# A conformer block on one core: convolution norm and activation through the convolution's PSUM banks, and another order of products in the first chunk

## The chip, the cores and the metric

The kernel runs on one core of a Trainium2 chip. The metric is the device time of one execution in microseconds (us), as the median of several runs. TensorE (PE) multiplies matrices out of SBUF into PSUM; ScalarE (ACT) and VectorE (DVE) read and write both; GpSimd (POOL) works in SBUF alone; SyncE (SP) issues the DMAs. PSUM has eight banks of 128 x 512 fp32 values.

## The reference

One layer on 256 positions of width 1024, all in float32:

```python
x = x + 0.5 * swiglu(rms_norm(x, ffn1_norm), ffn1_w_gate, ffn1_w_up, ffn1_w_down)
proj = rms_norm(x, mix_norm) @ w_in
conv_a, conv_b, q, k, v, gate_a, gate_b = jnp.split(proj, SPLITS, axis=-1)
u = causal_depthwise_conv(conv_a * jax.nn.sigmoid(conv_b), conv_dw, conv_dw_bias)   # 31 taps
u = jax.nn.silu(layer_norm(u, conv_ln_gain, conv_ln_bias))
y_a = u @ w_conv_proj
y_b = moba_attention(rms_norm(q), rms_norm(k), v) @ w_attn_proj      # 16 heads; 256 positions: one causal block
x = x + (jax.nn.sigmoid(gate_a) * y_a + jax.nn.sigmoid(gate_b) * y_b) @ w_out
x = x + 0.5 * swiglu(rms_norm(x, ffn2_norm), ffn2_w_gate, ffn2_w_up, ffn2_w_down)
```

## The kernel before

**Products.** Every fp32 operand is split in two fp32r parts, `hi` (rounded) and `lo` (the rest), for weights and for activations. A product of two operands is three matmuls: activation hi by weight hi (L165), activation hi by weight lo (L166), activation lo by weight hi (L167); in the first chunk, `gemm_first`, these are L132, L133 and L134. The program names the activation parts hTh and hTl, oh and ol (attention output), u2h and u2l (convolution output), mTh and mTl.

**Weights.** `gemm` makes one chunk of 512 output columns for both halves t of the 256 positions. It takes the weight in pieces of two times 128 rows: SP loads `raw` (512 KB), ACT casts it to `hi` (L100), DVE or POOL subtracts to get `lo` (L102), and PE issues 24 / 2 = 12 matmuls per piece. `raw`, `hi` and `lo` are rings of five buffers, so a load waits until `hi` and `lo` of the piece five earlier have been made. The first chunk is loaded in eight smaller pieces, each with a slice of x, which ACT (L125, hTh) and DVE (L126, hTl) scale and split.

**PSUM.** Three rings share the eight banks: `acc` (3 banks, the accumulators of `gemm`), `cv` (2) and `tr` (3, transposes and attention). In the kernel before, `cv` holds the accumulators of the first chunk and later those of the depthwise convolution, two channel blocks at a time; convolution works on DVE (L347) with its first tap on ACT (L343), and its result is copied back to `uT0` to `uT3` (L350).

**Norm and activation of the convolution.** `conv_norm` transposes `uT` to positions on partitions (16 transposes, L359, four in a bank), ACT copies each bank to `ynat` (L364), DVE takes statistics (L368, L370), ACT and POOL make the reciprocal root (L185, L187), and DVE normalizes `ynat` (L375); all this once for each half t. `conv_act` transposes back (16 transposes, L385; a bank needs both halves), ACT applies Silu with gain and bias into `z` (L392) and casts to `u2h` (L398), DVE subtracts to get `u2l` (L399).

**The order around it.** Python code is written as one sequence; `conv` and `conv_norm` are generators that `pump` advances a step at a time between weight pieces. The build's scheduler then lays the instructions out on each engine by an estimated timeline, under the data's dependencies and the rings' free buffers; each engine runs its list in order. Attention is eight blocks of `score` (L465), `flip` (L512, with copies L515) and `value` (L529, with L220 and L221 into oh and ol), all in the `tr` ring. The two chunks of `w_attn` follow, whose results are multiplied by the sigmoid of gate_b (L703, L714); then two chunks of `w_conv` (reading u2h and u2l) with gate_a (L722, L723); then `w_out` and the second feed-forward. ACT needs a table load when it changes between Exp, Sigmoid and Silu; `issue_after` keeps those groups apart: gate_b's sigmoids come after attention's last cast, the Silus after them, and gate_a's sigmoids after the instruction that `conv_act` returns.

Of the kernel before, what the change touches and what calls it, by code (L numbers as in the profile page):

```python
# [20 lines left out]
KD = D // P  # L21
# [7 lines left out]
CH = 512  # L29
# [21 lines left out]
class Build:  # L51
# [54 lines left out]
    def gemm_first(self, x0, w0, rest, hT):  # L106

        nc = self.nc
        acc = [self.cv(), self.cv()]
        hTh, hTl = hT  # L110
        ah, al = self.parts(*hT)
        for k in range(KD):
            raw = self.wp.tile([P, KP * CH], F32, tag="raw", name="raw", bufs=RAW_BUFS)
            hi = self.wp.tile([P, KP * CH], F32R, tag="hi", name="hi", bufs=HI_BUFS)
            lo = self.wp.tile([P, KP * CH], F32R, tag="lo", name="lo", bufs=LO_BUFS)
            if k == 0:
                nc.sync.dma_start(x0, self.io["x0"])
                nc.sync.dma_start(raw[:, :CH], w0)
                xk = x0[:, KD:]
            else:  # L120
                self.last_dma = nc.sync.dma_start(raw[:, : CH + S], rest[:, k - 1, :])
                xk = raw[:, CH : CH + S]
            g = x0[:, k : k + 1]
            sl = slice(k * S, (k + 1) * S)
            nc.scalar.activation(hTh[:, sl], xk, AF.Copy, scale=g)  # L125
            nc.vector.scalar_tensor_tensor(  # L126
                hTl[:, sl], xk, g, hTh[:, sl].bitcast(F32), ALU.mult, ALU.subtract
            )
            self.split(raw[:, :CH], hi[:, :CH], lo[:, :CH], False)
            for t in range(2):  # L130
                o, st, sp = acc[t], k == 0, k == KD - 1
                nc.tensor.matmul(o, ah(k, t), hi[:, :CH], start=st, stop=False)  # L132
                nc.tensor.matmul(o, ah(k, t), lo[:, :CH], start=False, stop=False)  # L133
                nc.tensor.matmul(o, al(k, t), hi[:, :CH], start=False, stop=sp)  # L134
        return acc

    def gemm(self, w, c, n, kt, ah, al, pump=0, pool=0.0, split_k=None, side=None):
# [214 lines left out]
    def conv_norm(self, yT, ynat):  # L352
        nc = self.nc
        for t in range(2):
            for c0 in range(0, KD, 4):
                ps = self.tr()
                for q in range(4):
                    c = c0 + q
                    nc.tensor.transpose(  # L359
                        ps[:, q * P : (q + 1) * P],  # L360
                        yT[c // 2][:, (c % 2) * S + t * P : (c % 2) * S + (t + 1) * P],
                        self.ident,
                    )
                nc.scalar.copy(ynat[:, t * D + c0 * P : t * D + (c0 + 4) * P], ps)  # L364
                yield 1
            st = self.tmp.tile([P, 2, 6], F32, tag="bst", name="bst", bufs=2)
            for c in range(2):
                nc.vector.bn_stats(st[:, c, :], ynat[:, t * D + c * CH : t * D + (c + 1) * CH])  # L368
            mv = self.tmp.tile([P, 2], F32, tag="mv", name="mv", bufs=2)
            nc.vector.bn_aggr(mv, st)  # L370
            r = self.rsqrt_mean(mv[:, 1:2], 1, 1)
            yield 1
            for c in range(2):
                y = ynat[:, t * D + c * CH : t * D + (c + 1) * CH]
                nc.vector.tensor_scalar(y, y, mv[:, 0:1], r, ALU.subtract, ALU.mult)  # L375
            yield 1

    def conv_act(self, ynat, hi, lo, after):
        nc = self.nc
        cst = self.cst  # L380
        for c in range(0, KD, 2):
            ps = self.tr()
            for q in range(2):
                for t in range(2):
                    nc.tensor.transpose(  # L385
                        ps[:, q * S + t * P : q * S + (t + 1) * P],
                        ynat[:, t * D + (c + q) * P : t * D + (c + q + 1) * P], self.ident,
                    )
            z = self.tmp.tile([P, CH], F32, tag="junk", name="z", bufs=2)
            with self.tc.issue_after(after.ins):  # L390
                for q in range(2):
                    last = nc.scalar.activation(  # L392
                        z[:, q * S : (q + 1) * S], ps[:, q * S : (q + 1) * S], AF.Silu,
                        bias=cst[:, C_LB + c + q : C_LB + c + q + 1],
                        scale=cst[:, C_LG + c + q : C_LG + c + q + 1],
                    )
            h = hi[:, c * S : (c + 2) * S]
            nc.scalar.copy(h, z)  # L398
            nc.vector.tensor_tensor(lo[:, c * S : (c + 2) * S], z, h.bitcast(F32), ALU.subtract)  # L399
        return last  # L400


    def head_norm(self, acc, rstd, c, dst, gain, rq=None):
# [437 lines left out]
```

## Time and profile before

| | |
|---|---|
| median of 3 runs | 647.08 us (646.92 to 647.13) |
| profiled execution | 647.48 us, its span 645.6 us |
| busy share of PE, DVE, ACT, POOL | 98%, 57%, 56%, 26% |
| matmul records on PE | 2952 |
| HBM read | 113.40 MB, 177 GB/s over the span |

The span is what the profiler saw from first to last instruction; the rest of an execution's time lies around it. Shares are means over the span. PEclk in the profile is the clock granted to TensorE, 1.00 being 2.4 GHz and 0.50 being 1.2 GHz. A busy PE is not a PE at its peak: the ends of matmuls are modelled, and back-to-back matmuls overlap in the rows.

### The profile page before, as it was taken

The numbers are of one execution on the slowest core, as the hardware profiler recorded it, in microseconds if no ns is written. First come the engines' busy times: TensorE is split into PE (matmuls) and PEld (weight loads), VectorE is DVE, ScalarE is ACT, GpSimd is POOL, SyncE is SP. The second block draws the span as 40 slices with busy tenths as digits, with TensorE's granted clock in tenths as the row PEclk, the third lists the DMA queues.
The fourth block names the chain that finished last, engine by engine and source line by source line (L and its number), as shares of the span: only waits on it lengthen the run. The fifth ranks groups of instructions, "written<-read, shape, count | busy, mean of one in ns | idle before, by whom it ended". The sixth has DMA issues, their size and how long they took to land.

```text
span 645.6 us, 8133 instructions
## 1 busy us (share of the span) xinstructions
PE 634.2 (98%) x2952; PEld 516.8 (80%) x2952; DVE 369.9 (57%) x625; ACT 362.5 (56%) x547; POOL 164.9 (26%) x83
## 2 busy tenths in 40 slices
PE   9999999999999999999999997899999999999997
PEld 7788888888888888777777785788888888888886
DVE  5655464554542699879313936485664546465541
ACT  6755354443545676987876667744655435444330
POOL 0100000000006999689866761000100000000000
PEclk9999999999999999999999999799999999999999
DMA  8966556567564555545654552264755656556630
GB/s 271 354 232 192 199 173 195 160 198 219 174 201 135 178 170 180 171 130 169 196 158 135 164 168 96 96 199 153 224 163 186 196 177 198 189 168 200 197 124 32
DMA packets 32855, 114.97 MB, mean 178 GB/s; under 512 B 3632, under 2 KB 4912, under 8 KB 32816
## 3 DMA queue, kind: packets, MB, share of 16 engines
q1 hardware_dynamic: 32816, 114.46, 55.9%
q8 instruction: 23, 0.38, 0.2%
q14 instruction: 16, 0.13, 0.1%
HBM read 113.40 MB, written 1.05 MB: 177 GB/s over the span
## 4 chain that ended last, share of the span: by engine, by line
PE 64%; DVE 2%; ACT 1%; issue 0%; DVEq 0%
PE acc L165 20%; PE acc L166 20%; PE acc L167 19%; PE tr L465 1%; PE tr L211 1%; PE tr L529 1%; PE tr L512 1%; DVE lo L102 1%; PE tr L438 1%; DVE bst L368 0%; ACT gate_b L703 0%; ACT z L392 0%; PE tr L655 0%; DVE gate_b L714 0%; ACT L703 0%
## 5 line engine op out<-in xcount | busy, mean ns | idle before, releaser
L100 ACT CAST hi<-raw 128x1024 fp32r<-128x1024 f32 (+1 forms) x216 | 223.1, 1035 | 220.3 <-PE acc L167 184.4
L102 DVE TENSOR_TENSOR lo<-raw,hi 128x1024 fp32r<-128x1024 f32 (+1 forms) x156 | 186.2, 1197 | 167.2 <-ACT hi L100 162.7
L102 POOL TENSOR_TENSOR lo<-raw,hi 128x1024 fp32r<-128x1024 f32 x60 | 143.7, 2420 | 200.3 <-ACT hi L100 200.2
L347 DVE SCALAR_TENSOR_TENSOR cv<-uT,cst,cv 128x255 f32<-128x255 f32 (+28 forms) x240 | 95.2, 465 | 8.4 <-ACT cv L343 8.2
L166 PE MATMUL acc<-lo,h1h 128*128 128x512 f32 x224 | 88.3, 394 | 0.0
L165 PE MATMUL acc<-hi,h1h 128*128 128x512 f32 x224 | 88.0, 398 | 0.2 <-DVE un L646 0.2
L167 PE MATMUL acc<-hi,h1l 128*128 128x512 f32 x224 | 87.3, 393 | 0.0
L165 PE MATMUL acc<-hi,h2h 128*128 128x512 f32 x176 | 69.1, 393 | 0.0
L165 PE MATMUL acc<-hi,aTh 128*128 128x512 f32 x176 | 68.8, 391 | 0.0
L167 PE MATMUL acc<-hi,aTl 128*128 128x512 f32 x176 | 68.5, 389 | 0.0
L166 PE MATMUL acc<-lo,aTh 128*128 128x512 f32 x176 | 68.5, 389 | 0.0
L166 PE MATMUL acc<-lo,h2h 128*128 128x512 f32 x176 | 68.5, 390 | 0.0
L167 PE MATMUL acc<-hi,h2l 128*128 128x512 f32 x176 | 67.2, 390 | 0.0
L166 PE MATMUL acc<-lo,hTh 128*128 128x512 f32 x160 | 62.4, 390 | 0.5 <-DVE lo L102 0.5
L165 PE MATMUL acc<-hi,hTh 128*128 128x512 f32 x160 | 62.2, 392 | 0.0
L167 PE MATMUL acc<-hi,hTl 128*128 128x512 f32 x160 | 62.2, 389 | 0.0
L165 PEld LDWEIGHTS acc<-hi,h1h 128*128 128x128 f32 x224 | 42.1, 188 | 10.3 <-issue 0.7
L167 PEld LDWEIGHTS acc<-hi,h1l 128*128 128x128 f32 x224 | 42.1, 188 | 9.3 <-issue 0.7
L166 PEld LDWEIGHTS acc<-lo,h1h 128*128 128x128 f32 x224 | 42.1, 188 | 8.9 <-issue 0.8
L167 PEld LDWEIGHTS acc<-hi,aTl 128*128 128x128 f32 x176 | 33.0, 188 | 6.9
L165 PEld LDWEIGHTS acc<-hi,aTh 128*128 128x128 f32 x176 | 33.0, 188 | 6.8
L165 PEld LDWEIGHTS acc<-hi,h2h 128*128 128x128 f32 x176 | 33.0, 188 | 6.8
(138 smaller groups left out, 778.8 us busy)
## 6 DMA issues: line engine op xcount, KB each, us to landing
raw<-w_in SPq DMA_DIRECT2D x56, 512.0 KB, 4.2
raw<-w2gu SPq DMA_DIRECT2D x44, 512.0 KB, 4.4
raw<-w1gu SPq DMA_DIRECT2D x40, 512.0 KB, 4.8
raw<-w1d SPq DMA_DIRECT2D x22, 512.0 KB, 4.3
raw<-w2d SPq DMA_DIRECT2D x22, 512.0 KB, 4.4
raw<-w_attn SPq DMA_DIRECT2D x8, 512.0 KB, 4.2
raw<-w_conv SPq DMA_DIRECT2D x8, 512.0 KB, 4.0
raw<-w_out SPq DMA_DIRECT2D x8, 512.0 KB, 4.4
```

The costliest lines, as they stand in the source:

```text
L100: nc.scalar.copy(hi, raw)
L102: ins = eng.tensor_tensor(lo, raw, hi.bitcast(F32), ALU.subtract)
L165: nc.tensor.matmul(o, ah(k, t), wh, start=st, stop=False)
L166: nc.tensor.matmul(o, ah(k, t), wl, start=False, stop=False)
L167: nc.tensor.matmul(o, al(k, t), wh, start=False, stop=sp)
L211: nc.tensor.transpose(ps[:, q * S + t * P : q * S + (t + 1) * P], src(t, j + q), self.ident)
L347: nc.vector.scalar_tensor_tensor(o, u, w, o, ALU.mult, ALU.add)
L438: nc.tensor.transpose(ps[:, q * S + t * P : q * S + (t + 1) * P], xs[t][:, (j + q) * P : (j + q + 1) * P], self.ident,)
L465: ins = nc.tensor.matmul(ps[q][:, t * P : t * P + (t + 1) * P], qT[r, b * S + t * P : b * S + (t + 1) * P], kT[r, b * S : b * S + (t + 1) ...
L512: nc.tensor.transpose(ps[:, i * P : (i + 1) * P], pr[:, o : o + P], self.ident)
L529: ins = nc.tensor.matmul(ps[q * HD : (q + 1) * HD, kt * P : S], v[:, kt * D + h * HD : kt * D + (h + 1) * HD], pT[:, o : o + n], start=kt ...
```

## The change

Two edits. In `gemm_first` both products with the weights' hi part come first for both halves, and those with the weights' lo part last. In `conv_norm` and `conv_act` the transposes go into the `cv` ring instead of the `tr` ring, and `conv_act` returns its last cast to `u2h` instead of its last Silu.

```diff
@@ gemm_first
             for t in range(2):
-                o, st, sp = acc[t], k == 0, k == KD - 1
-                nc.tensor.matmul(o, ah(k, t), hi[:, :CH], start=st, stop=False)
-                nc.tensor.matmul(o, ah(k, t), lo[:, :CH], start=False, stop=False)
-                nc.tensor.matmul(o, al(k, t), hi[:, :CH], start=False, stop=sp)
+                nc.tensor.matmul(acc[t], ah(k, t), hi[:, :CH], start=k == 0, stop=False)
+                nc.tensor.matmul(acc[t], al(k, t), hi[:, :CH], start=False, stop=False)
+            for t in range(2):
+                nc.tensor.matmul(acc[t], ah(k, t), lo[:, :CH], start=False, stop=k == KD - 1)
@@ conv_norm
-                ps = self.tr()
+                ps = self.cv()
@@ conv_act
-            ps = self.tr()
+            ps = self.cv()
...
-                    last = nc.scalar.activation(
+                    nc.scalar.activation(
...
-            nc.scalar.copy(h, z)
+            rounded = nc.scalar.copy(h, z)
...
-        return last
+        return rounded
```

The build lays out other lists for PE, DVE and ACT from it; those of POOL and SP stay the same. On PE, in the second chunk of `w_attn` (products of `oh` and `ol`), the first transposes of `conv_norm` (L359) stand now between the products of an early piece; a line with + is new at this place:

```order
 L165 MATMUL acc<-hi,oh 128x512
 L166 MATMUL acc<-lo,oh 128x512
+L359 MATMUL cv<-ident,uT_1535 128x128 x2
+L359 MATMUL cv<-ident,uT_1536 128x128 x2
 L167 MATMUL acc<-hi,ol 128x512
 L165 MATMUL acc<-hi,oh 128x512
 L166 MATMUL acc<-lo,oh 128x512
+L359 MATMUL cv<-ident,uT_1537 128x128 x2
+L359 MATMUL cv<-ident,uT_1538 128x128 x2
 L167 MATMUL acc<-hi,ol 128x512
```

Before, they came later, behind attention's last `value` group.

The transposes of `conv_act` (L385) stood before as one group of 16 behind all products of `w_attn`. Now PE has them in three groups, of which this is the part from the first to the second, still among products of `w_attn`; 24 more products and then the last eight transposes follow it:

```order
L385 MATMUL cv<-ident,ynat 128x128 x2
L165 MATMUL acc<-hi,oh 128x512
L166 MATMUL acc<-lo,oh 128x512
L165 MATMUL acc<-hi,oh 128x512
L166 MATMUL acc<-lo,oh 128x512
L165 MATMUL acc<-hi,oh 128x512
L166 MATMUL acc<-lo,oh 128x512
L167 MATMUL acc<-hi,ol 128x512 x3
L385 MATMUL cv<-ident,ynat 128x128 x6
L165 MATMUL acc<-hi,oh 128x512
```

So products of `w_attn` now stand behind transposes that need the normalized `ynat`.

On ACT, from attention's last casts on, before:

```order
L220 CAST oh<-tr 128x256
L703 ACT_TABLE_LOAD
L703 ACTIVATE gate_b<-gate_b 128x512 x4
L364 COPY ynat<-tr 128x512 x3
L100 CAST hi<-raw 128x1024
L364 COPY ynat<-tr 128x512
L100 CAST hi<-raw 128x1024 x2
L185 ACTIVATE ms<-mv 128x1
L100 CAST hi<-raw 128x1024 x2
L185 ACTIVATE ms<-mv 128x1
L392 ACT_TABLE_LOAD
L392 ACTIVATE z<-tr,cst 128x256 x4
```

and after the change:

```order
L364 COPY ynat<-cv 128x512 x2
L185 ACTIVATE ms<-mv 128x1
L220 CAST oh<-tr 128x256
L703 ACT_TABLE_LOAD
L703 ACTIVATE gate_b<-gate_b 128x512 x4
L100 CAST hi<-raw 128x1024
L392 ACT_TABLE_LOAD
L392 ACTIVATE z<-cv,cst 128x256 x4
L398 CAST u2h<-z 128x512
L100 CAST hi<-raw 128x1024
L398 CAST u2h<-z 128x512
L100 CAST hi<-raw 128x1024 x3
```

The copies to `ynat` and the steps of the norm moved ahead of gate_b's table load, and four of the piece casts (L100) moved behind the first Silus.

## Rows read from the trace of the kernel before

**Rows 1.** The page, first part: busy us (share of the span) and instructions.

```profile
PE 634.2 (98%) x2952; PEld 516.8 (80%) x2952; DVE 369.9 (57%) x625; ACT 362.5 (56%) x547; POOL 164.9 (26%) x83
```

**Rows 2.** Windows: length, busy PE, PEld, DVE, ACT, POOL, granted clock, DMA, GB/s.

```profile
0.00:17.00 17.00, 15.91 (x66) 12.31 (x66) 9.61 (x19) 10.56 (x19) 1.44 (x10) 1.00 0.85 276
400.00:410.00 10.00, 5.39 (x20) 4.01 (x20) 6.88 (x11) 6.01 (x11) 1.97 (x2) 0.69 0.71 238
409.00:410.00 1.00, 1.00 (x3) 0.79 (x3) 0.89 (x2) 0.70 (x3) 0.00 (x0) 0.50 0.00 0
420.00:640.00 220.00, 220.00 (x1010) 182.43 (x1009) 119.77 (x127) 99.53 (x120) 1.64 (x1) 1.00 0.56 174
```

**Rows 3.** Timeline of PE, 380 to 411: start, busy, what [idle before <-releaser].

```profile
380.37 0.39 PE L165 MATMUL acc<-hi,oh 128*128 128x512 f32 x1
...
382.05 0.87 PE L529 MATMUL tr<-pT,v 128*64 128x256 f32 x8
382.85 0.88 PE L512 MATMUL tr<-ident,pr 128*128 128x128 f32 x6
...
388.59 1.09 PE L359 MATMUL tr<-ident,uT 128*128 128x128 f32 x8
...
393.11 0.66 PE L359 MATMUL tr<-ident,uT 128*128 128x128 f32 x4 [0.43 <-ACT ynat L364]
394.43 0.50 PE L165 MATMUL acc<-hi,oh 128*128 128x512 f32 x1 [0.66 <-DVE gate_b L714]
...
399.78 0.39 PE L167 MATMUL acc<-hi,ol 128*128 128x512 f32 x1
401.50 0.76 PE L385 MATMUL tr<-ident,ynat 128*128 128x128 f32 x3 [1.33 <-ACT ms L185]
405.18 3.13 PE L385 MATMUL tr<-ident,ynat 128*128 128x128 f32 x13 [2.93 <-DVE ynat L375]
408.62 0.80 PE L165 MATMUL acc<-hi,u2h 128*128 128x512 f32 x1 [0.30 <-ACT u2h L398]
...
410.76 0.39 PE L166 MATMUL acc<-lo,u2h 128*128 128x512 f32 x1
```

**Rows 4.** Timeline of the start: the first chunk and the second's first piece.

```profile
5.30 0.19 PEld L133 LDWEIGHTS cv<-lo,hTh 128*128 128x128 f32 x1 [0.43 <-DVE lo L102]
...
9.91 0.33 SPq L151 DMA_DIRECT2D raw<-w1gu  x1
...
15.24 1.05 ACT L100 CAST hi<-raw 128x1024 fp32r<-128x1024 f32 x1 [2.24 <-PE cv L134]
...
17.60 0.50 PE L166 MATMUL acc<-lo,hTh 128*128 128x512 f32 x1 [0.53 <-DVE lo L102]
```

**Rows 5.** DMA issues, 9.8 to 10.2: count, KB, us to landing.

```profile
raw<-w1gu SPq DMA_DIRECT2D x1, 512.0 KB, 5.2
```

**Rows 6.** Timeline of ACT, POOL and DVE, 379 to 408, as in rows 3.

```profile
379.57 2.10 ACT L100 CAST hi<-raw 128x1024 fp32r<-128x1024 f32 x2
...
389.10 1.28 ACT L703 ACT_TABLE_LOAD   x1
390.39 2.19 ACT L703 ACTIVATE gate_b<-gate_b 128x512 f32<-128x512 f32 x4
...
394.86 0.60 ACT L364 COPY ynat<-tr 128x512 f32<-128x512 f32 x1
...
406.12 1.93 ACT L392 ACTIVATE z<-tr,cst 128x256 f32<-128x256 f32 x4 [3.43 <-PE tr L385]
...
380.70 4.74 POOL L102 TENSOR_TENSOR lo<-raw,hi 128x1024 fp32r<-128x1024 f32 x2 [0.58 <-ACT hi L100]
...
401.48 1.88 POOL L187 TENSOR_TENSOR rs<-ms,neghalf 128x1 f32<-128x1 f32 x1 [1.38 <-ACT ms L185]
...
393.09 0.69 DVE L368 BATCH_NORM_STATS2 bst<-ynat 128x6 f32<-128x512 f32 x1 [3.55 <-ACT ynat L364]
...
404.59 1.00 DVE L375 TENSOR_SCALAR ynat<-ynat,mv,rs 128x512 f32<-128x512 f32 x2
```

## The prediction

> **What bounds the kernel now.** I read the page's first part first: TensorE (PE) is busy 634.2 of 645.6 us [rows 1], so time can only come out of the 11.4 us in which it is not, or out of stretches in which it runs slowly. The windows show where that is: from 420 to 640 us PE is busy all 220 us, but from 400 to 410 only 5.39 of 10, and the mean granted clock there is 0.69 [rows 2]. That is the seam between the attention projection and the convolution projection.
>
> The timeline of PE then tells the seam apart [rows 3]. The last `w_attn` product starts at 399.78. Then PE has nothing but the 16 transposes of L385, which need the normalized convolution output: three go out at 401.50, the other 13 at 405.18 after 2.93 us idle on DVE's L375, and the first product with `u2h` starts at 408.62. Two smaller waits lie ahead: 0.43 us before the last L359 transposes (393.11) and 0.66 us for a product (394.43). The gap also costs clock: from 409 to 410 the granted clock is 0.50, the 1.2 GHz level [rows 2], and the five products from 408.62 to 410.76 take 2.14 us [rows 3].
>
> Why the norm is late stands in the queues of the other engines [rows 6]. The L359 transposes go into the `tr` ring, which attention is using, so they are issued behind attention's last block. The copies of `ynat` stand on ACT behind a table load (389.10) and gate_b's sigmoids (390.39, 2.19 us); the last ends at 394.86 + 0.60 = 395.46. From there to the end of the last normalization, 404.59 + 1.00 = 405.59, are 10.1 us, because DVE's small steps stand between `lo` subtractions.
>
> The other edit is in the first chunk. A weight load of PE there waits 0.43 us for DVE's `lo` [rows 4]; such waits are all that the new order of products can remove.
>
> **The change, part by part.**
>
> *First chunk.* The hi and low-activation products now come first and those with `lo` last. The 48 products and their operands are the same; four products instead of two now stand ahead of the first that needs `lo`. What counts is when the second chunk can go on. Its first piece is issued at 9.91 us [rows 4] and lands 5.2 us later [rows 5], at 15.1; ACT's cast starts at 15.24 and takes 1.05 us, DVE's subtraction follows, and PE's first `lo` product starts at 17.60 after 0.53 us idle [rows 4]. The profile names PE as releaser of the cast at 15.24, but the landing ends at the same moment, and the landing doesn't depend on PE. So PE will finish the first chunk some 0.4 us sooner and stand that much longer before 17.60. Value: 0, with bounds 0 and 0.5 (if PE was what released the cast).
>
> *Norm transposes in the `cv` banks.* The convolution has finished with these two banks before 381 us. On PE the first eight L359 transposes move from behind attention's last value group to the first piece of its second chunk, directly after the product at 380.37 and its successor; the other eight follow attention's last flip. Up to 380.37 both programs issue the same on every engine, apart from the first chunk. From there to the first `u2h` product the changed program issues 60 products, two value groups (L529), one flip group (L512), 16 transposes of L359 and 16 of L385. Prices: a product 0.233 us (394.43 to 399.78 are 23 steps, 5.35 us); a value group 0.80 (382.05 to 382.85); the flip 0.88; eight transposes 1.09 (the busy time at 388.59, which covers the change back to products) [rows 3]. Sum: 60 x 0.233 + 1.60 + 0.88 + 4 x 1.09 = 20.8 us, so 401.2 if PE never waits.
>
> Does it wait? I replay the other queues with the durations of before [rows 6]. ACT is free of its casts at 379.57 + 2.10 = 381.67 and copies the first half at once. GpSimd (POOL) works on its last `lo` until 380.70 + 4.74 = 385.44, and the power for the first half comes behind it: 1.88 at most, 387.3. DVE normalizes (1.00) to 388.3, takes the second half's statistics (2 x 0.69 by 393.09, and an estimated 0.4 for two steps on a few elements) to 390.1; the power ends by 392.0 and the normalization by 393.0. PE reaches the transposes that need it at 380.37 + 36 products (8.39) + 1.60 + 0.88 + 18 transposes (2.45) = 393.7: 0.7 us to spare.
>
> Then ACT, from 390.1: cast of `oh` 0.4 (a quarter of a piece, priced above its share), table load 1.28, four sigmoids 2.19, one cast 1.05, table load 1.28, four Silus 1.93, cast to `u2h` 0.55 (half a piece's 1.05): 398.8, against PE's 401.2. The second half follows after one cast, one `u2h` cast, three casts (1.05 each), Silu 1.93 and `u2h`: 406.1. PE needs it 25 products after 401.2, at 407.0: 0.9 us to spare.
>
> *A rule on table loads.* Both loads stand on that path. The table-load row of before lasts 1.28 us, and the sigmoids start 0.01 us after its end [rows 6]. The Trainium skill (ScalarE: Activation LUTs, What ACT_TABLE_LOAD costs) adds a drain of about 1.38 us to each switch of the set. By that page the chain would be 2.8 us longer, the second half ready at 408.9 instead of 406.1, PE would stand 1.9 us, and the sum would be 640.4, an estimate. The rows here show no drain, so the sum goes without it.
>
> *`rounded` in place of `last`.* gate_a's sigmoids now wait for the last `u2h` cast instead of standing ahead of the last two. The casts come sooner; the sigmoids end near 410, and gate_a's first product is not multiplied before 412. Value 0; the cover is the 48 products of the first convolution chunk (11.2 us); without it the 2.19 us would show.
>
> *Sum.* PE reaches the `u2h` products at 401.2 instead of 408.62: 7.4 us. With no long gap the clock stays at 1.00, and the first five products take 5 x 0.233 = 1.2 instead of 2.14: 1.0 us. Together 8.4. From 420 to 640 us PE has no idle time in before [rows 2], so nothing there can absorb the shift: it reaches the end whole. The profiled execution took 647.48 us (span 645.60 and 1.88 around it), 0.40 above the median of 647.08. 647.48 - 8.4 = 639.1; on the scale of the median 638.7. Since I priced the transposes and the flip with their busy times, which hold some overlap, I take 638.5. No more than about 9.5 can be won: the waits of [rows 3], the slow transposes and products, and 0.5 at the start. That gives 637.
>
> **The rivals.**
>
> *ACT comes late (0.15).* Its margins of 0.7 to 0.9 us are thin, and ACT now has piece casts between Silu and the second half. For it: they wait for landings and for free `hi` buffers too. Against it: SP's order is unchanged and the buffers come free earlier. If two handoffs of the chain take 1 to 2 us more, PE stands as long: 640 to 642. One such way has 0.04 of the 0.15: if ACT stood after each of the two table loads for as long as the load itself, 1.28 us, the second half would come at 408.7 against 407.0, 1.7 us of wait: 640.2. (The page's drain, above, is of this kind; the 0.01 us behind the load at 389.10 speaks against it.)
>
> *The norm passes stay as slow as now (0.06).* If the second half needs 10.1 us from copy to normalized as in before, it is ready at 397.8 (PE's second group of L359 ends at 380.37 + 12 products + 16 transposes + 0.80 + 0.88 = 387.0, a copy takes 0.60, then 10.1) while PE stands from 393.7 on: 4.1 us, and perhaps 2 us at the lower clock: 643 to 645. Against it: the subtractions that stood between the steps now come after them on DVE.
>
> *Slower (0.03).* The same wait, further: the transposes are now in the middle of the `w_attn` products, so 24 products stand behind them on the in-order PE and can't cover it as they do now. From a wait of some 6.5 us with the lower clock behind it, that is with the second half normalized at 400.2 or later, the gain is gone; 9 us of wait would give 649. It would need a queue on DVE or POOL that the order of the changed program doesn't show.
>
> *Nothing moves (0.03).* PE loses its clock in the first chunk, where its short waits are now gathered into one before each cast: 48 products at some 0.43 us (2.14 / 5, [rows 3]) would cost 9.5 us, less the 0.53 us in which PE stands at 17.60 anyway: 9.0 against 8.4, 647 to 648. Against it: in before PE is idle 1.09 of the first 17 us, and the granted clock is 1.00 throughout [rows 2]; the change adds some 0.4.
>
> **How the numbers follow.** The likeliest case, the seam closed, has 0.73: 638.5, own range 637 to 640. ACT late, 0.15, reaches to 642; the slow norm, the slower case and no change share 0.12, and I leave those outside. Range 637.0 to 641.8. A measurement of this kernel can tell about 0.2%, 1.3 us, from no change. Faster: 0.73 + 0.15 + 0.06 = 0.94; same 0.03; slower 0.03.
>
> **What would show it.** Right: PE's L385 in three groups (2, 6, 8), with the first `u2h` product between 400 and 402 us and the windows at 1.00 from 390 to 420; the L359 transposes at 381 to 387 us; the first `lo` product of the second chunk still near 17.6. Wrong in the norm: an idle PE before the group of six, released by DVE L375. Wrong in ACT: an idle PE before a `u2h` product. Wrong on the first chunk: the second chunk's `lo` product before 17.3 us, or a granted clock below 1.00 ahead of 20 us.

## The result

The changed kernel takes 638.93 us (median, 638.39 to 639.39) where the kernel before takes 647.11 beside it: ratio 0.987, 95% interval 0.985 to 0.989, 8.2 us faster. The forecast was 638.5, range 637.0 to 641.8, with 0.94 on faster.

The first part of the page of the changed kernel, to be read against [rows 1]:

```profile
PE 630.4 (99%) x2952; PEld 515.3 (81%) x2952; DVE 370.6 (58%) x625; ACT 362.2 (57%) x547; POOL 162.7 (26%) x83
```

PE has the same 2952 records and 3.8 us less busy time: before, the late transposes and the products at the lower clock counted longer. Its waits, the whole list (what waited, on what; us in total, times, longest):

```profile
PE acc L165 <- ACT hi L100: 1.2, 1, 1.2
PE tr L574 <- DVE idle L571: 1.1, 1, 1.1
PE acc L166 <- DVE lo L102: 0.5, 1, 0.5
PE cv L131 <- ACT hi L100: 0.3, 1, 0.3
PE acc L165 <- DVE un L646: 0.2, 1, 0.2
```

None of the L385 and `ynat` waits of [rows 3] is left; what stands here is the warm-up, the first 20 us and one short wait in the input projection (`w_in`). The windows say the same (length, busy PE, PEld, DVE, ACT, POOL, granted clock, DMA, GB/s):

```profile
390.00:400.00 10.00, 10.00 (x54) 8.10 (x53) 4.89 (x8) 9.07 (x14) 0.55 (x1) 1.00 0.16 49
400.00:410.00 10.00, 10.00 (x50) 8.36 (x49) 8.42 (x10) 9.97 (x16) 0.00 (x0) 1.00 0.63 193
410.00:420.00 10.00, 10.00 (x46) 8.29 (x45) 7.28 (x9) 4.54 (x7) 0.00 (x0) 1.00 0.61 213
```

From 400 to 410 PE is busy all 10 us at clock 1.00; in [rows 2] it was 5.39 us at 0.69. PE's timeline through the seam (381.65 is the same product as 380.37 in [rows 3]):

```profile
381.65 0.39 PE L165 MATMUL acc<-hi,oh 128*128 128x512 f32 x1
382.11 0.60 PE L359 MATMUL cv<-ident,uT 128*128 128x128 f32 x4
...
385.05 0.87 PE L512 MATMUL tr<-ident,pr 128*128 128x128 f32 x6
385.68 0.48 PE L166 MATMUL acc<-lo,oh 128*128 128x512 f32 x1
...
386.93 1.03 PE L359 MATMUL cv<-ident,uT 128*128 128x128 f32 x8
387.72 0.48 PE L165 MATMUL acc<-hi,oh 128*128 128x512 f32 x1
...
392.27 0.38 PE L385 MATMUL cv<-ident,ynat 128*128 128x128 f32 x2
...
394.55 0.82 PE L385 MATMUL cv<-ident,ynat 128*128 128x128 f32 x6
...
400.69 1.04 PE L385 MATMUL cv<-ident,ynat 128*128 128x128 f32 x8
401.48 0.48 PE L165 MATMUL acc<-hi,u2h 128*128 128x512 f32 x1
...
402.72 0.39 PE L166 MATMUL acc<-lo,u2h 128*128 128x512 f32 x1
```

No row carries a wait, L385 stands in groups of 2, 6 and 8, and the first `u2h` product follows 19.83 us after the product at 381.65; before it was 28.25. The five steps behind it take 1.24 us, where [rows 3] have 2.14.

ACT, POOL and DVE in the same stretch, to be read against [rows 6]:

```profile
391.26 1.28 ACT L703 ACT_TABLE_LOAD   x1
392.55 2.19 ACT L703 ACTIVATE gate_b<-gate_b 128x512 f32<-128x512 f32 x4
...
395.70 1.28 ACT L392 ACT_TABLE_LOAD   x1
397.00 1.93 ACT L392 ACTIVATE z<-cv,cst 128x256 f32<-128x256 f32 x4
398.81 0.63 ACT L398 CAST u2h<-z 128x512 fp32r<-128x512 f32 x1
...
405.44 0.64 ACT L398 CAST u2h<-z 128x512 fp32r<-128x512 f32 x1
...
390.04 0.55 POOL L187 TENSOR_TENSOR rs<-ms,neghalf 128x1 f32<-128x1 f32 x1 [2.82 <-ACT ms L185]
...
391.27 0.42 DVE L221 TENSOR_TENSOR ol<-tr,oh 128x256 fp32r<-128x256 f32 x1 [1.55 <-ACT oh L220]
391.61 0.99 DVE L375 TENSOR_SCALAR ynat<-ynat,mv,rs 128x512 f32<-128x512 f32 x2
```

The second half is normalized at 392.60, and PE wants it at 394.55. The start, against [rows 4]:

```profile
16.50 1.04 ACT L100 CAST hi<-raw 128x1024 fp32r<-128x1024 f32 x1 [3.03 <-PE cv L134]
...
15.83 0.62 PE L134 MATMUL cv<-lo,hTh 128*128 128x512 f32 x2
17.60 0.73 PE L165 MATMUL acc<-hi,hTh 128*128 128x512 f32 x2 [1.15 <-ACT hi L100]
18.86 0.50 PE L166 MATMUL acc<-lo,hTh 128*128 128x512 f32 x1 [0.53 <-DVE lo L102]
```

In this execution the second chunk's first `lo` product starts 1.26 us later than in [rows 4]. So the span, which fell by 8.0 us (645.6 to 637.6), hides a seam worth more. The table cuts each profiled span in three: up to that `lo` product (start), from there to the first `u2h` product (middle), and the rest (end).

| kernel | start | middle | end | span |
|---|---|---|---|---|
| before | 17.60 | 391.02 | 236.98 | 645.6 |
| after | 18.86 | 382.62 | 236.12 | 637.6 |
| after, again | 17.83 | 382.63 | 236.14 | 636.6 |
| first chunk alone | 17.70 | 391.05 | 236.55 | 645.3 |
| `cv` ring and `rounded`, old first chunk | 17.30 | 382.61 | 236.09 | 636.0 |
| norm in `cv`, activation in `tr` | 18.15 | 382.70 | 235.95 | 636.8 |
| norm in `tr`, activation in `cv` | 18.12 | 391.31 | 236.47 | 645.9 |
| `rounded` alone | 17.80 | 391.03 | 236.17 | 645.0 |
| `cv` ring, last Silu returned | 18.05 | 382.65 | 237.70 | 638.4 |
| after, two copies more on ACT | 17.85 | 382.73 | 236.52 | 637.1 |
| after, four copies more on ACT | 17.45 | 384.82 | 239.83 | 642.1 |
| after, six `raw` and four `lo` buffers | 16.52 | 386.36 | 236.02 | 638.9 |

Between the first two rows the middle is 8.40 us shorter (391.02 to 382.62) and the end 0.86, which is the lower clock. That clock reaches into the middle too: the 13 transposes at 405.18 in [rows 3] take 3.13 us of busy time, where eight take 1.04 in the changed kernel; so a part of the 8.40 is the lower clock as well. How long it lasts differs between executions that have the same waits. In before:

```profile
403.00:404.00 1.00, 0.00 (x0) 0.00 (x0) 1.00 (x2) 0.00 (x0) 0.35 (x1) 0.88 1.02 397
...
410.00:411.00 1.00, 1.00 (x5) 0.76 (x4) 0.00 (x0) 1.00 (x3) 0.00 (x0) 0.71 0.00 0
```

and in the profiled execution of `rounded` alone:

```profile
405.00:406.00 1.00, 0.60 (x3) 0.60 (x4) 0.80 (x2) 0.00 (x0) 0.00 (x0) 0.62 0.88 320
...
408.00:409.00 1.00, 0.70 (x4) 0.30 (x3) 0.19 (x1) 1.00 (x3) 0.00 (x0) 0.67 0.45 184
```

Between the two windows the clock is 0.50, some 7 us in before and some 3.5 in the other. The five executions without a wait in the middle (the changed kernel twice, and the three with part of the change that hold L359 in `cv`) agree there to 0.1 us; their starts differ by 1.6.

### The profile page after: what moved, and what is told of

It reads as the page before. It is cut to its first block, busy times and chain, and to the rows that moved or that the text cites. A ratio compares the mean times of both kernels' runs of the same rounds, so it can differ in the third digit from the quotient of the medians.

```text
span 637.6 us, 8138 instructions
## 1 busy us (share of the span) xinstructions
PE 630.4 (99%) x2952; PEld 515.3 (81%) x2952; DVE 370.6 (58%) x625; ACT 362.2 (57%) x547; POOL 162.7 (26%) x83
## 4 chain that ended last, share of the span: by engine, by line
PE 67%; DVE 0%; DVEq 0%; issue 0%
PE acc L165 20%; PE acc L166 20%; PE acc L167 20%; PE tr L465 1%; PE tr L211 1%; PE tr L529 1%; PE tr L512 1%; PE tr L438 1%; PE tr L655 0%; PE cv L385 0%; PE cv L359 0%; DVE un L646 0%; DVE ot L754 0%; DVEq L830 0%
## 5 line engine op out<-in xcount | busy, mean ns | idle before, releaser
L100 ACT CAST hi<-raw 128x1024 fp32r<-128x1024 f32 (+1 forms) x216 | 222.8, 1035 | 218.4 <-PE acc L167 182.8
```

The source lines that it names most:

```text
L100: nc.scalar.copy(hi, raw)
```

## The experiments

Three batches, each with its own runs of the kernel before, whose medians were 647.80, 647.85 and 648.03 (single runs 646.0 to 649.5). Ratios are to the same batch.

**Which edit.** Six kernels take the change apart. *The first chunk alone* (kernel before with the new order of products in `gemm_first`):

> Only the new order of products in the first chunk, everything else as before; the lists of ACT, DVE, POOL and SP are then the same as before. My theory (the second chunk waits for its first piece, which arrives by DMA whatever PE does): PE finishes the first chunk some 0.4 us sooner, stands that much longer before the second chunk, and the time is that of before within 0.3 us. Rival 1 (PE was what released the first cast of the second chunk): 0.3 to 0.5 us faster. Rival 2 (the order itself costs, as the changed kernel's profile, in which the second chunk's first lo product starts 1.26 us later than before, could suggest): 0.5 to 1.3 us slower, with that product at 18.5 us or later in every profile.

Measured: 648.01 us, ratio 1.0000 (0.9988 to 1.0011). The seam's waits are those of before. The first `lo` product of the second chunk starts at 17.70. The edit is worth nothing that 0.7 us could show; Rival 1's 0.3 to 0.5 us lies inside that interval, and what speaks against it is the landing, told further below.

*The other edit alone*, the first chunk as in before:

> Only the norm and activation in the convolution's banks with the returned last cast; the first chunk as before. ACT, DVE, POOL and SP issue as in the changed kernel. My theory: the whole gain is here; from the product that follows 38 products of the second w_attn chunk's row to the first u2h product PE needs 19.8 us instead of 28.25, and the clock adds 1.0: 8.5 to 9.4 us faster than before. Rival (the first chunk's order carries part of the gain, or takes part of it back): 8.0 or less, or the changed kernel's 8.2 exactly with the first chunk at 0.

Measured: 637.82, ratio 0.984 (0.983 to 0.986). This is the whole gain: 10.0 us below before in its batch, more than the 8.5 to 9.4 expected. The profiled pair has 8.41 in the middle and 0.89 at the end; a part of the rest lies in the runs of before, told in the next section.

*Which of the two rings.* In the changed kernel with the old first chunk, one ring goes back at a time:

```diff
 # e5: conv_norm in cv, conv_act in tr
@@ conv_act
-            ps = self.cv()
+            ps = self.tr()
 # e6: conv_norm in tr, conv_act in cv
@@ conv_norm
-                ps = self.cv()
+                ps = self.tr()
```

> conv_norm's transposes in the cv banks, conv_act's left in the tr banks, the returned last cast kept, first chunk as before. My theory (what matters is that conv_norm needn't queue behind attention for a tr bank, so that copies, statistics and normalization come before gate_b's table load): nearly the whole gain, 8 to 9.4 us. Rival (two rings are needed because conv_act's own transposes stand behind attention as well): half or less, 2 to 5 us.

> The reverse: conv_norm's transposes stay in the tr banks, conv_act's go to the cv banks, the returned last cast kept, first chunk as before. The scheduler leaves all 16 transposes of conv_act in one group behind the products of w_attn. My theory: no gain, within 0.5 us of before, with PE idle some 3 us on DVE L375 and the granted clock at 0.50 around 409 us as before. Rival (conv_act's bank matters by itself): 2 to 5 us faster.

Measured: 638.53 (0.985, 0.984 to 0.987) with `conv_norm` in `cv`, and 648.13 (1.000, 0.999 to 1.001) with `conv_act` there. The longest of PE's waits in the second kernel:

```profile
PE cv L385 <- DVE ynat L375: 4.6, 2, 3.3
```

The old wait for `ynat` is there in full; only its bank is another. So the gain comes from where L359 may stand on PE, and the ring of L385 gives nothing.

*The value returned by `conv_act`.* In the kernel before, `rounded` instead of `last`; and the changed kernel (old first chunk) with `last`:

```diff
 # e4, on the kernel before; e3 is the reverse on the changed one
-                    last = nc.scalar.activation(
+                    nc.scalar.activation(
...
-            nc.scalar.copy(h, z)
+            rounded = nc.scalar.copy(h, z)
...
-        return last
+        return rounded
```

> The kernel before with the returned last cast alone: gate_a's table load and sigmoids behind the last two u2h casts, all transposes in the tr banks. My theory (in the kernel before PE had other products to do while these casts came late): no change, within 0.4 us of before. Rival (the returned cast is worth the 1.2 to 1.7 us that it is worth with the transposes in the cv banks): 1 us or more faster than before.

> Both sets of transposes in the cv banks, but conv_act returns its last Silu as before, so gate_a's table load and sigmoids stand ahead of the last two u2h casts; first chunk as before. My theory (with the seam closed the returned cast is no longer free): the third u2h cast ends at about 409.6 us on the scale of the changed kernel's profile while PE asks for it near 408.4, after 30 products; PE idle about 1.2 us before a u2h product, and the time 1 to 1.5 us above the kernel with both. Rival (the returned cast is worth nothing, as I put it in the prediction): the same time within 0.4 us.

Measured: `rounded` alone 647.02, ratio 0.9994 (0.998 to 1.001): nothing. `last` in the closed seam 640.25 (0.988, 0.986 to 0.989), where the changed kernel in the same batch has 637.99 (0.984, 0.983 to 0.986): 2.3 us slower, where 1 to 1.5 were expected. ACT and PE of the kernel with `last`:

```profile
404.82 1.28 ACT L703 ACT_TABLE_LOAD   x1
406.11 2.19 ACT L703 ACTIVATE gate_a<-gate_a 128x512 f32<-128x512 f32 x4
408.21 0.60 ACT L398 CAST u2h<-z 128x512 fp32r<-128x512 f32 x1
...
407.39 0.39 PE L167 MATMUL acc<-hi,u2l 128*128 128x512 f32 x1
408.86 0.50 PE L165 MATMUL acc<-hi,u2h 128*128 128x512 f32 x1 [1.09 <-ACT u2h L398]
409.20 0.39 PE L166 MATMUL acc<-lo,u2h 128*128 128x512 f32 x1
```

gate_a's table load and sigmoids stand ahead of the last two casts to `u2h`, and PE stands 1.09 us. The end is 1.6 us longer than in the changed kernel; the clock stays at 1.00 through this wait:

```profile
408.00:409.00 1.00, 0.14 (x1) 0.14 (x2) 0.16 (x1) 1.00 (x3) 0.00 (x0) 1.00 0.93 369
```

Counted from start to start, the wait is longer than its row says: 1.47 us from 407.39 to 408.86, and 0.34 to the next product, where a step is 0.23. Together that is 1.35 of the 1.6. What the medians show beyond 1.6 is less than the 1.6 by which the starts differ, but its cause is not shown; the lower clock is not it, as the mean granted clock is 0.999 or 1.000 in all four executions.

**How much cover there is.** *The changed kernel once more*, for a second measure of it:

> The changed kernel once more, beside the runs below. My theory (the seam gives 9.3 us, and the spread of single executions comes from when the second chunk's first piece lands): within 0.3% of the kernel with the norm edit alone (637.8), 637.5 to 638.9 in the median, with the first lo product of the second chunk anywhere from 17.2 to 18.9 us and the span minus that start at 618.7. Rival (the first chunk's order takes back a microsecond): 638.7 to 639.4 again, the lo product at 18.4 or later.

Measured: 637.99, ratio 0.984 (0.983 to 0.986), 0.9 us below its first median; seam and end are the same to 0.02 us in the table, and the start is 1.03 us earlier. *Copies of a zero tile onto itself* put a delay on ACT between gate_b's sigmoids and the Silus; the kernel's own work is all there, but the build also moves piece casts ahead of the first cast to `u2h`, one with two copies and two with four:

```diff
+        pad = self.const.tile([P, CH], F32, name="pad")
+        nc.gpsimd.memset(pad, 0.0)
...
         last = sigmoid(gb, self.last_att)
+        for _ in range(2):        # 4 in the other kernel
+            with tc.issue_after(last.ins):
+                last = nc.scalar.copy(pad, pad)
```

> The changed kernel with two extra copies on ACT instead of four, one piece cast ahead of the first u2h cast. My theory (ACT has about 2 us to spare at the first u2h product): the first u2h cast ends 2.2 us later than in the changed kernel, within 0.3 us of when PE asks for it; PE idle 0 to 0.5 us there, the granted clock stays at 1.00, the time within 0.6 us of the changed kernel (638.0). Rival (any delay on ACT's chain comes through): 2 us slower.

> The changed kernel with four extra copies of 128x512 on ACT (a tile of zeros onto itself, 0.5 to 0.6 us each) between gate_b's sigmoids and the Silus; the scheduler also puts two piece casts ahead of the first u2h cast. My theory (ACT's chain has about 2 us to spare at the first u2h product and no more): the first u2h cast ends near 403.5 us on the scale of the changed kernel's profile, PE is idle 2 to 2.5 us before its first u2h product, and the time is 2 to 2.8 us above the changed kernel. Rival (PE is not near ACT's chain): no change.

Measured: two copies 639.23 (0.987, 0.986 to 0.989), four copies 641.99 (0.991, 0.990 to 0.993). Two copies take 1.25 us busy on ACT, the piece cast beside them 1.06. With two, middle and end are 0.1 and 0.4 us longer: the cover is just used up. The median is 1.2 us above the changed kernel's in the other batch, where at most 0.6 was expected; the trace places 0.5 of it. With four, PE shows two waits, of which the first was expected at 2 to 2.5 us:

```profile
399.26 1.28 PE L385 MATMUL cv<-ident,ynat 128*128 128x128 f32 x8
402.27 0.50 PE L165 MATMUL acc<-hi,u2h 128*128 128x512 f32 x1 [1.74 <-ACT u2h L398]
...
403.14 0.63 PE L166 MATMUL acc<-lo,u2h 128*128 128x512 f32 x1
404.41 0.79 PE L167 MATMUL acc<-hi,u2l 128*128 128x512 f32 x1 [0.64 <-DVE u2l L399]
...
409.99 0.39 PE L167 MATMUL acc<-hi,u2l 128*128 128x512 f32 x1
```

Its windows show what follows:

```profile
403.00:404.00 1.00, 0.77 (x3) 0.03 (x1) 1.00 (x2) 1.00 (x2) 0.00 (x0) 0.50 0.86 221
...
405.00:409.00 4.00, 4.00 (x11) 3.12 (x10) 2.83 (x3) 2.74 (x6) 0.00 (x0) 0.50 0.81 249
409.00:410.00 1.00, 1.00 (x5) 0.76 (x4) 0.70 (x1) 0.98 (x3) 0.00 (x0) 0.60 0.88 242
```

Waits of 2.4 us cost this execution 5.9 us in middle and end (384.82 + 239.83 against 382.63 + 236.14). Counted from start to start the two waits are 3.3: the first `u2h` product comes 3.01 us after the start of the L385 group, in the changed kernel 0.79, and 1.27 us lie between 403.14 and 404.41 instead of 0.23. The other 2.6 are the lower clock: it is at 1.2 GHz from 403 until past 409, and the 13 steps from 404.41 to 409.99 take 5.58 us, where 13 steps of 0.23 are 3.0. The median is only 4.0 us above the changed kernel's (2 to 2.8 were expected), and this execution, at 643.97, is the slowest of five. The record has the mean granted clock of each: 0.995 here, 0.997 in the one at 641.73 us, and 1.000 in the three at 641.98 to 642.34. So in these three the lower clock did not follow, and they lose some 4 us all the same. Only this execution has a trace; 3.3 us of the 4 are what the waits cost here from start to start.

**The start.** What is left is a wait of PE for the second chunk's first piece. Three kernels, all on the changed one, try to move it. *A smaller first piece*:

```diff
-                        u = self.gemm(wgu, c, n, KD, ah, al)
+                        u = self.gemm(wgu, c, n, KD, ah, al, split_k=[1, 1])
```

> The changed kernel with the first piece of the second chunk cut in two of 128 rows (256 KB each), so that the cast (0.6 instead of 1.05 us), the subtraction (0.7 instead of 1.2) and the landing are shorter. My theory (the start ends when that piece has landed, been cast and been subtracted): the second chunk's first lo product starts 1 to 1.7 us sooner and the time is 0.8 to 1.5 us below the changed kernel. Rival (the later pieces of the chunk, bound by the same DMA and the ring of five buffers, take it back): the same time, with PE idle at a later piece instead.

Measured: 639.40 (0.987, 0.985 to 0.988), 1.4 us slower than the changed kernel in its batch. Expected was 0.8 to 1.5 us faster. PE's first `lo` product of the chunk comes at 17.43, 0.4 us before that of the changed kernel's second profile, and then PE waits for a later piece:

```profile
20.07 0.73 PE L165 MATMUL acc<-hi,hTh 128*128 128x512 f32 x2 [0.21 <-ACT hi L100]
21.33 0.50 PE L166 MATMUL acc<-lo,hTh 128*128 128x512 f32 x1 [0.52 <-DVE lo L102]
```

*The new order of products in the second chunk too* (in `gemm`, for that chunk alone, eight products with `hi` and then the four with `lo` of each piece):

> The changed kernel with the first chunk's order of products also in the second chunk: in each piece eight products with the weights' hi part, then the four with lo. My theory (the wait for lo that is left stands at the second chunk's first piece, where only two products stand ahead of it): PE's 0.53 us before that lo product vanishes, the chunk goes on 0.5 to 1.2 us sooner, and the time is 0.4 to 1.2 us below the changed kernel beside the same start. Rival (the next pieces land too late to use it, as when the first piece was cut in two): the same time, PE idle at the second or third piece.

Measured: 638.18 (0.986, 0.984 to 0.987), no better than the changed kernel in the other batch. The wait for `lo` is gone, and from the chunk's first product to the first `u2h` product it takes 383.06 us (17.54 to 400.60) against 383.89 (16.57 to 400.46). But in this execution the first product itself came 0.97 us later, so the 0.8 doesn't show in the time.

*One `raw` buffer more, one `lo` buffer less* (`RAW_BUFS, HI_BUFS, LO_BUFS = 6, 5, 4` instead of 5, 5, 5):

> The changed kernel with six buffers for raw pieces and four for lo, so that a load waits for the piece six earlier. My theory (the second chunk's first piece is issued when DVE has subtracted the piece four before it, near 9.9 us): it is issued 1 to 1.5 us sooner and lands 0.3 to 1 us sooner, since the DMA engines are nearly full until then; the time is 0.3 to 1 us below the changed kernel, unless four lo buffers make DVE or POOL wait for PE later on. Rival (the start is bound by the DMA engines' rate alone): no change, or slower by the smaller lo ring.

Measured: 641.29 (0.991, 0.989 to 0.992), 3.1 us above the kernel just told, in the same batch. The start is the best of all: the loads are issued from 8.03 us, the first cast starts at 13.16, and PE goes from the first chunk to the second without a wait, the first `lo` product at 16.52. The seam takes back more. PE, and a window behind its wait:

```profile
393.75 1.12 PE L385 MATMUL cv<-ident,ynat 128*128 128x128 f32 x4 [2.89 <-ACT z L392]
```

```profile
394.00:395.00 1.00, 1.00 (x5) 1.00 (x5) 0.00 (x0) 1.00 (x3) 0.00 (x0) 0.50 0.74 283
```

With other buffers the build laid the lists out another way: the third bank of L385 stands early among `w_attn`'s products. `cv` has two banks, so it waits until a Silu has read the first, and that Silu stands behind gate_b's sigmoids on ACT. The middle is 3.7 us longer: 2.9 of wait and a stretch at 1.2 GHz (0.50 in the window from 394); the mean granted clock is 0.996 or 0.997 in all five executions. The better start together with the changed kernel's seam was not tried.

## Why the prediction came out as it did

**The seam.** Right in its mechanism: the waits for `ynat` went, the steps of the norm moved ahead of gate_b's sigmoids, and the two kernels with one ring each show that L359's place alone did it. The term was mis-sized by 1.0: middle 8.4 instead of 7.4 us. The working priced eight transposes at 1.09, their busy time, and the flip at 0.88; from start to the next start they take 0.79 (386.93 to 387.72) and 0.63 (385.05 to 385.68). Four groups and a flip are 1.5 us less, of which 0.5 is spent again, at least in part by products behind transposes, whose first step is 0.32 us (387.72 to 388.04) instead of 0.23. I had allowed for this overlap by 0.2 us. The clock's share was 0.86 for 1.0 against the execution of [rows 3]; the other three executions with the old seam have ends of 236.17 to 236.55, 0.05 to 0.43 above the changed kernel's. The least is `rounded` alone, where the clock is back before 409.

**The sum.** In the profiled executions seam and clock are 8.4 to 9.3 us where 8.4 was forecast. The profiled pair doesn't show it, because its starts differ by 1.26 the other way; and the medians of the changed kernel, 638.93 and 637.99, lie on both sides of 638.5. Beside their own runs of before, the medians are 9.9 us (the changed kernel, second measure) and 10.0 us (the norm edit alone) lower, more than the 9.5 that the prediction allowed at most. A part of that is the lower clock, which I took as fixed in before: of its 49 runs in the three batches, 14 have a mean granted clock of 0.997 and a median of 647.1 us, 27 have 0.995 and 647.9, and seven have 0.993 and 648.6 (one has 0.996). The forecast started from 647.08, the median of three runs. So 638.5 came as near as it did by some luck: the gain was taken too small, and so was the time of before; the start I took as fixed.

**The first chunk.** Right at 0, as far as 0.7 us can tell. But that PE finishes the chunk some 0.4 us sooner is not borne out. In before its last product is

```profile
16.17 0.39 PE L134 MATMUL cv<-hi,hTl 128*128 128x512 f32 x1
```

and ends at 16.56; in the changed kernel it ends at 15.83 + 0.62 = 16.45, 0.1 sooner, and over the twelve profiled executions with the old pieces and five `raw` buffers at 16.2 to 17.3 with the new order and 16.6 to 17.1 with the old. The 1.15 us ahead of the product at 17.60 are there because the cast starts at 16.50 instead of 15.24. What released the cast was the landing: the profile names the DMA as its releaser in 9 of the twelve, in the changed kernel the piece lands 6.7 us after its issue at 9.68, 0.1 us before the cast, and with a sixth `raw` buffer the cast came 2 us sooner than in before (13.16).

**`rounded` at 0.** This step failed, though the sum didn't rest on it, as the replay had the casts in their new order. The cover that I named, 48 products, is for gate_a's sigmoids coming late. The other side was not looked at: with `last` they come early, ahead of the casts that PE waits for. In before, where PE is late anyway, that costs nothing (ratio 0.9994); in the closed seam it costs 1.6 us of span and 2.3 of median.

**ACT late.** It didn't happen, and its margins were mis-stated a little: 2.0 us at the first `u2h` (399.44 against 401.48; forecast 2.4), and 1.2 in the second half (406.08 against 407.26; forecast 0.9). The kernels with copies show that the case was real and close, and dearer than I priced it, since I gave a wait of 1 to 2 us its own length: waits that the rows give as 2.4 us are 3.3 from start to start and went with 4.0 us in the median, and in the profiled execution the lower clock came on top. The subcase of a stand after each table load fell: the Silus start 0.02 us after the load at 395.70 ends. The drain of the Trainium skill (ScalarE: Activation LUTs, What ACT_TABLE_LOAD costs) is not in the rows, and the estimate of 640.4 was 1.5 to 2.4 too high.

**The norm stays slow; slower.** Neither. From the second half's last copy to its normalization it took 4.0 us (388.64 to 392.60) instead of 10.1, as no piece's `lo` subtraction stood between the steps any more; the power on POOL, too, took 0.55 instead of 1.88. There were 2.0 us of margin where 0.7 was forecast.

**Nothing moves.** It fell: the granted clock is 1.00 over the first 17 us, with PE idle for 2.0 of them:

```profile
0.00:17.00 17.00, 15.04 (x64) 12.32 (x64) 9.13 (x18) 10.09 (x19) 1.44 (x10) 1.00 0.84 271
```

## What to carry to other kernels

When an engine waits late in a stage, ask which buffer ring placed the work that it waits for: here 16 small transposes were held behind attention by sharing its ring, and moving them to two idle banks was worth some 9 to 10 us, while the ring of the consuming transposes was worth nothing. An edit that measures as nothing beside a large stall can be worth microseconds once the stall is gone, so measure it again in the new kernel. Price groups of small matmuls from start to next start, and compare kernels by stretches between two events in the program when the start varies by as much as the effect; and look at the granted clock of every run, as a kernel with a long wait can lose a different amount to it each time.

## What the runs showed of the hardware

- The first piece's landing varies from one execution to the next: from its issue to the cast it took 6.82 us (9.68 to 16.50) and 5.66 (9.81 to 15.47) in the two profiled executions of the changed kernel, whose spans differ by 1.0 with the same middle and end; in the kernel with the old first chunk it took 5.04 (9.90 to 14.94).
- A wait of PE can be followed by 1.2 GHz or not, and for longer or shorter. One of 1.09 us left the clock at 1.00. The one of 2.89 us was followed by some 3 us at 1.2 GHz. With four copies on ACT the profiled execution shows some 6 us at 1.2 GHz behind waits of 1.74 and 0.64 us, while three of the five executions have a mean granted clock of 1.000. In the old seam the same waits (1.3 and 2.9 us) went with some 7 us in before and some 3.5 in `rounded` alone. What sets this was not tested.
- The power on 128 elements on POOL took, as the profile dates it, 0.54 to 0.56 us in all 20 rows of the ten profiled kernels that hold L359 in `cv`, where DVE stood idle beside it (in the changed kernel from 389.72 to 391.27), and 1.34 or 1.88 to 1.89 in the eight rows of the four with the old seam, where DVE was on a piece's `lo` subtraction (in before from 398.48 and from 401.72). That DVE's work is the cause was not tested.
